# Six second-stage units by seven products in place of three, in a one-core attention layer

## The chip, the cores and the metric

The kernel runs on one core of a Trainium2 chip. The metric is the device time of one execution in microseconds (us); lower is better. The engines that appear below are TensorE (PE in the profile: matrix products; PEld is its loading of weights), VectorE (DVE), ScalarE (ACT), GpSimd (POOL) and SyncE (SP), whose queue issues the DMAs.

## The reference

One layer of an encoder trunk over 2048 tokens of width 1024, in float32: RMSNorm, one input projection to queries, keys, values and a gate (1024 columns each, 16 heads of 64), neighbourhood attention, gating by SiLU, output projection, residual, final RMSNorm.

```python
h = rmsnorm(x, norm_0)
q, k, v, gate = split(h @ w_in_0, 4)            # 2048 x 1024 each
# tokens form a 32 x 64 grid; a query sees the 8 rows x 16 columns around it
s = q . k / 8 + rpb_0[head, row offset, column offset]   # others: -1e30
o = softmax(s) @ v
x = x + (o * silu(gate)) @ w_out_0
return rmsnorm(x, norm_f)
```

`rmsnorm(x, g)` is `x * rsqrt(mean(x*x) + 1e-6) * g`. The factor `rsqrt(...)` belongs to a token, `g` to a column of x.

## The kernel before

**Precision.** Each float32 operand of a product is split into a high part (a rounded copy, made by ScalarE) and a low part (the operand minus the copy, made by VectorE). A product a*b is then three matmuls: high*high, high*low, low*high. `split_to` and `use_item` make such splits; a tile is mostly 128 x 512.

**Seven products.** The input projection of queries, keys and gate (`q`, `k`, `g`) is cut into 12 units (three kinds, four column groups j). In `seven_products` a unit is a 2 x 2 block product by Strassen's scheme in Winograd's form: seven block products of 12 matmuls each (84), line 421, in place of eight (96). It needs sums of weight blocks (`sum_`, line 410), sums of input blocks (T1 to T4, made once for all units), the splits of both (`form`, lines 403 and 404), and sums of results (`keep`, `add`, `out_`: lines 428, 432, 438). `form` runs six products ahead of the matmul that uses it. x blocks are named by their place: B11, B21, B12, B22, where the second digit is the block of 512 tokens.

**The norm.** x is multiplied by g (`g0`, per partition) when it is split. The token factor is applied to the results: `rb[c]`, a 128 x 512 tile made by `diagonal` and `spread_rstd`, is multiplied in by `evac` (VectorE, lines 326 and 328) for a plain result and by `out_` (POOL, line 439) for a summed one; for values `evac_v` takes it as a scale (line 377).

**The stages.**
- Stage one (to 326 us): the values of the first 1024 tokens, then all 12 units of `q`, `k`, `g` for those tokens by seven products (`stage_one`).
- Stage two (326 to 471 us): the values of the other 1024 tokens (`pair`), then three units (j = 0) by seven products (`stage_two`, `units_two`).
- Stage three: 64 attention steps (`scores`, `normalise`, `turns`, `values`), each for two of the four column blocks of a pair of heads `p` and a band of rows `T`. The 16 steps of band 0 come first, then 32 of bands 1 and 2, then 16 of band 3. Between them TensorE is fed with filler: first the remaining nine units in plain form (`projections`, lines 365, 367, 369; `halves` is their order), then the output projection (`outputs`, lines 1223 to 1227).

**A step.** The order of the instructions is written out by hand; each engine works its own queue in order. Step i does: `begin` (POOL adds position bias and mask to tables `em`, line 945, six sums when the head pair or band type changes; loads for later steps are queued), `feed` (filler matmuls), `middle`, `feed`, `normalise` of step i-1 (reciprocal on VectorE, line 979; scaling on POOL, line 981), `turns` of step i-2 (transposes, line 986; copies to `pta` on VectorE and ScalarE, lines 1011 and 1010), `scores` of step i (line 963; VectorE adds the table and finds the minimum, line 970; ScalarE takes the exponential, line 973) and `values` of step i-2 (line 1031). After the second half of a head pair the result is multiplied by the gate (`og`, line 1045) and stored. The amount of filler is fixed:

```python
early = 96 * (12 - len(units_two)) + 192
amount = [early / 48] * 48 + [(384 - 30) / 18] * 18
```

so a step in the first 48 has (96 x 9 + 192)/48 = 22 matmuls of filler. The loop over the steps is

```python
    for i in range(N + 2):
        a = amount[i]
        begin(i)
        feed(a * 0.45)
        middle(i)
        feed(a * 0.55, 8)
        if 0 < i <= N:
            normalise(i - 1)
        if i > 1:
            turns(i - 2)
        ...
        if i < N:
            scores(i)
        if i > 1:
            values(i - 2)
```

`later_loads(fs, lag, step)` issues loads that many filler matmuls later.

**Splits in the steps.** Filler needs splits of weights (`use_item`, line 178; output weights line 183). The queries of a step are split by `split_q` (line 499), gated results by `split_og` (line 1104). Four blocks of x that stage two overwrites are loaded and split again at the start of stage three (lines 155 and 156).

## Time and profile before

| | us |
|---|---|
| median of 3 runs | 1101.96 (1101.08 to 1102.29) |
| the profiled execution | 1102.79 |
| its span, first to last instruction | 1101.0 |
| mean granted clock of TensorE | 0.99 |

In the profile an engine's busy time is the union of its instructions. A group's row reads: line, engine, operation, output <- inputs, shapes, count | busy us, mean ns of one | idle time of the engine just before them and what ended it. Matmuls overlap, so their mean is longer than their distance. A row of waits reads: who <- for whom: total us, times, longest.

### The profile page before, as it was taken

How to read it: one execution, taken by the hardware profiler on the slowest of the kernel's cores; microseconds unless marked ns; L12 is line 12 of the kernel's file. 1: busy time of each engine (PE TensorE's matmuls, PEld its weight loads, DVE VectorE, ACT ScalarE, POOL GpSimd, SP SyncE). 2: the span in 40 equal slices, each digit the busy share in tenths (PEclk: the TensorE clock that was granted, in tenths of full speed). 3: DMA queues.
4: the chain of work that ended last, by engine and by line, in shares of the span. 5: the costliest groups of instructions: out<-in, count | busy, mean ns of one | idle time of the engine just before them, and what ended most of it. 6: DMA issues, size and time to landing. Idle time of an engine off the chain costs nothing.

```text
span 1101.0 us, 22543 instructions
## 1 busy us (share of the span) xinstructions
PE 1080.7 (98%) x7657; PEld 883.6 (80%) x7657; DVE 732.7 (67%) x1663; ACT 531.5 (48%) x1336; POOL 378.5 (34%) x483
## 2 busy tenths in 40 slices
PE   9999999999999999999999999999999999999997
PEld 6888888888888888877888888888877888887885
DVE  5376778788777337575665766665777777776644
ACT  7545343343344433255554554564556555555422
POOL 0000312222130001245445444424447666675200
PEclk9999999999999999998999999999999999999999
DMA  8633545454574235587767878687979797887452
GB/s 307 209 96 105 185 132 181 143 173 112 166 216 138 80 89 157 195 263 232 233 193 241 251 223 230 211 268 222 259 237 286 228 288 225 252 274 211 152 153 77
DMA packets 142962, 217.29 MB, mean 197 GB/s; under 512 B 18048, under 2 KB 65408, under 8 KB 142848
## 3 DMA queue, kind: packets, MB, share of 16 engines
q1 hardware_dynamic: 142704, 215.58, 64.6%
q8 instruction: 62, 1.02, 0.4%
q14 instruction: 52, 0.43, 0.1%
q10 hardware_dynamic: 144, 0.26, 0.1%
HBM read 157.05 MB, written 58.72 MB: 196 GB/s over the span
## 4 chain that ended last, share of the span: by engine, by line
PE 88%; DVE 5%; DMA 3%; issue 2%; ACT 1%; POOL 1%; SPq 0%; DVEq 0%; POOLq 0%
PE pp L421 24%; PE pv L534 16%; PE o L1031 7%; PE s L963 6%; PE pp L369 6%; PE pp L367 6%; PE pp L365 5%; PE po L1227 5%; PE po L1223 4%; PE po L1225 4%; PE ph L986 4%; ACT x L973 1%; PE zp L1242 1%; DVE gl L1104 1%; DMA sgt<-sgd 0%
## 5 line engine op out<-in xcount | busy, mean ns | idle before, releaser
L981 POOL TENSOR_SCALAR x<-x,st 128x360 f32<-128x360 f32 (+5 forms) x256 | 143.1, 579 | 239.1 <-DVE st L979 157.1
L439 POOL TENSOR_TENSOR tmp<-tmp,rb 128x512 f32<-128x512 f32 x45 | 73.5, 1634 | 399.2 <-DVE tmp L438 358.4
L973 ACT ACTIVATE x<-x,st 128x360 f32<-128x360 f32 (+5 forms) x256 | 151.8, 594 | 56.4 <-DVE st L970 56.4
L421 PE MATMUL pp<-h,f 128*128 128x512 f32 x480 | 155.4, 389 | 0.0
L945 POOL TENSOR_TENSOR em<-e,mk 128x480 f32<-128x480 f32 (+5 forms) x160 | 140.8, 915 | 5.0 <-DVE st L970 5.0
L421 PE MATMUL pp<-t,f 128*128 128x512 f32 x540 | 129.8, 389 | 0.1
L970 DVE CUSTOM_DVE_ANT_0 x<-s,em 128x360 f32<-128x360 f32 (+5 forms) x256 | 123.8, 538 | 5.1 <-PE s L963 2.0
L421 PEld LDWEIGHTS pp<-t,f 128*128 128x128 f32 x540 | 101.3, 188 | 21.5 <-DVE u L432 0.6
L369 PE MATMUL pp<-h,w 128*128 128x512 f32 x288 | 115.9, 403 | 0.0
L367 PE MATMUL pp<-l,w 128*128 128x512 f32 x288 | 114.2, 397 | 0.0
L365 PE MATMUL pp<-h,w 128*128 128x512 f32 x288 | 113.6, 394 | 0.0
L1010 ACT ACTIVATE pta<-ph 96x256 f32<-96x256 f32 (+1 forms) x224 | 58.8, 333 | 105.8 <-PE ph L986 105.8
L1031 PEld LDWEIGHTS o<-pta,vt 96*64 96x64 f32 (+2 forms) x1792 | 86.0, 139 | 24.2 <-DVE pta L1011 10.2
L421 PEld LDWEIGHTS pp<-h,f 128*128 128x128 f32 x480 | 90.1, 188 | 18.8
L1031 PE MATMUL o<-pta,vt 96*64 96x128 f32 (+4 forms) x1792 | 95.2, 258 | 7.5 <-DVE pta L1011 4.6
L1227 PE MATMUL po<-wol,gh 128*128 128x512 f32 x252 | 101.4, 403 | 0.0
L1223 PE MATMUL po<-woh,gh 128*128 128x512 f32 x252 | 100.0, 397 | 0.0
L1225 PE MATMUL po<-woh,gl 128*128 128x512 f32 x252 | 99.7, 395 | 0.0
L1011 DVE COPY pta<-ph 128x384 f32<-128x384 f32 (+3 forms) x128 | 60.5, 513 | 51.5 <-PE ph L986 51.2
L421 PE MATMUL pp<-l,f 128*128 128x512 f32 x240 | 93.4, 389 | 0.0
L534 PE MATMUL pv<-wh,h 128*128 128x512 f32 x256 | 88.1, 390 | 0.0
L534 PE MATMUL pv<-wh,l 128*128 128x512 f32 x256 | 88.0, 389 | 0.0
(136 smaller groups left out, 1951.1 us busy)
## 6 DMA issues: line engine op xcount, KB each, us to landing
raw<-in_wg_dram SPq DMA_DIRECT2D x126, 256.0 KB
e<-in_rpb_dram SPq DMA_DIRECT2D x54, 240.0 KB
vt<-vd SPq DMA_DIRECT2D x256, 48.0 KB
row<-in_xr_dram SPq DMA_DIRECT2D x32, 256.0 KB
vd<-v SPq DMA_DIRECT2D x32, 256.0 KB
k_hi<-hi SPq DMA_DIRECT2D x32, 256.0 KB
k_lo<-lo SPq DMA_DIRECT2D x32, 256.0 KB
qd<-tmp SPq DMA_DIRECT2D x32, 256.0 KB
```

The lines of the kernel that those rows point to most:

```text
L365: nc.tensor.matmul(p, wh[w, b][:, cols], hh[k, c], start=(k == 0), stop=False)
L367: nc.tensor.matmul(p, wh[w, b][:, cols], hl[k, c], start=False, stop=False)
L369: nc.tensor.matmul(p, wl[w, b][:, cols], hh[k, c], start=False, stop=(k == NK - 1))
L421: nc.tensor.matmul(B[n, P], t[:, int(m == 2), c], x[k][int(m == 1)], start=P in (1, 6, 5) and k == 0 and m == 0, stop=k == 3 and m == 2, s ...
L534: nc.tensor.matmul(ps[t], a[:, o], b, start=k == 0 and m == 0, stop=k == NK - 1 and m == 2)
L945: (nc.gpsimd if attending[0] or not s else nc.vector).tensor_tensor(sh(t), E[p, s][:, u0 + 4:u1 + 4, v0 + 8:v1 + 8], sh(MK[0][:, m0:m0 + n ...
L973: nc.scalar.activation(X[i, C][s], X[i, C][s], AF.Exp, bias=st[:, s:s + 1], scale=-1.0, accum_out=st[:, 2 + s:3 + s])
L981: nc.gpsimd.tensor_scalar(X[i, C][s], X[i, C][s], st[:, 4 + s:5 + s], 0.5, op0=OP.mult, op1=OP.mult)
L1031: nc.tensor.matmul(o[s * 64:s * 64 + 64, C * 128 + q0:C * 128 + q0 + nq], vt[C][:k, g - g0_, s * 64:s * 64 + 64], t[:k, at:at + nq], start ...
L1223: nc.tensor.matmul(p, gh, woh[q, j], start=(i == 0), stop=False)
L1225: nc.tensor.matmul(p, gl, woh[q, j], start=False, stop=False)
L1227: nc.tensor.matmul(p, gh, wol[q, j], start=False, stop=(i == NK - 1))
```

## The change

- `units_two` holds j = 0 and 1: six units go by seven products in stage two, six stay in plain form. `halves` starts at j = 2. A step in the first 48 now has (96 x 6 + 192)/48 = 16 matmuls of filler.
- For the second 1024 tokens the token factor is multiplied into the x blocks before they are split and summed: the new `normed` (VectorE, one instruction with `g` and `rb`). Eight such multiplications stand in stage one (`norms`: two in the third-last unit, six in the second-last), eight in stage two, four at the start of stage three. For this `diagonal` and `spread_rstd` of blocks 2 and 3 come earlier, and the loads of x11 and x21 too.
- The results for these tokens then need no factor: `out_` leaves out POOL's multiplication, the plain result goes from PSUM to `give` without `evac`, `evac_v` scales by 1.0, and `flush` and `pending` go. The sums T1 to T4 lose their factors and one ScalarE copy each.
- The gate is kept in plain order; the product `og` reorders it while reading.
- `split_og` runs ahead only where `quiet` says that POOL has no table sums; the query split moves to the step before, into the odd steps. `qr` has a tile of another pool.
- Loads in a step: `vt` first, then bias tables, keys later, the gate last.

```diff
-    units_two = [(k, j) for j in range(1) for k in "kqg"]
-    halves = [(k, j, 1, c) for j in range(1, 4) for g in (("k", "q", "g") if j < 3 else ("k", "qg")) for c in (2, 3) for k in g]
+    units_two = [(k, j) for j in range(2) for k in "kqg"]
+    halves = [(k, j, 1, c) for j in range(2, 4) for g in (("k", "q", "g") if j == 2 else ("k", "qg")) for c in (2, 3) for k in g]
...
         if kind == "x":
-            split_x(a, b, t, (hh[a, b], hl[a, b]))
+            normed("x%d1" % (a // 4 + 1), b, a % 4, t)
+            split_to(hh[a, b], hl[a, b], t, None)
...
-    def give(kind, hp, c, tmp):
+    def give(kind, hp, c, t, psum=False):
...
         if kind == "q":
-            store(("q", hp, c), 12, lambda: nc.sync.dma_start(qd[hp][:, s], tmp))
+            if psum:
+                o = ev([128, 512], F32, "q")
+                nc.scalar.activation(blocked(o), tiled(t), AF.Copy)
+                t = o
+            store(("q", hp, c), 12, lambda: nc.sync.dma_start(qd[hp][:, s], t))
             return
...
             nc.vector.tensor_tensor(lay(tmp), of(B[n, P]), of(u), OP.add)
-            nc.gpsimd.tensor_tensor(lay(tmp), lay(tmp), of(rb[c]), OP.mult)
+            if c0 == 0:
+                nc.gpsimd.tensor_tensor(lay(tmp), lay(tmp), of(rb[c]), OP.mult)
...
+    def normed(f, c, k, t):
+        nc.vector.scalar_tensor_tensor(t, t, gain(f, k), rb[c], op0=OP.mult, op1=OP.mult)
...
+            if (n, i) == (-3, 1):
+                diagonal(2)
+            if (n, i) == (-3, 3):
+                spread_rstd(2)
+            if (n, i) in norms:
+                f, k = norms[n, i]
+                normed(f, 2, k, L2[f][k])
+            if (n, i) == (-3, 4):
+                diagonal(3)
...
+        norms = {(-2, 3): ("x11", 0), (-2, 5): ("x11", 1), (-1, 0): ("x11", 2), (-1, 1): ("x11", 3),
+                 (-1, 3): ("x21", 0), (-1, 4): ("x21", 1), (-1, 5): ("x21", 2), (-1, 6): ("x21", 3)}
...
                 for k in ks:
-                    split_to(*X2[f][k], x[k], gain(f, k))
+                    normed(f, 3, k, x[k])
+                    split_to(*X2[f][k], x[k], None)
...
-                    y = ev([128, 512], F32, "y")
                     a, b, c = x11[k], x12[k], x22[k]
-                    nc.scalar.activation(y, b, AF.Copy, scale=gain("x12", k))
+                    nc.vector.tensor_tensor(c, c, b, OP.subtract)
                     nc.vector.tensor_tensor(b, b, a, OP.subtract)
-                    nc.vector.scalar_tensor_tensor(c, c, gain("x22", k), y, op0=OP.mult, op1=OP.subtract)
-                    nc.vector.scalar_tensor_tensor(a, a, gain("x11", k), c, op0=OP.mult, op1=OP.add)
+                    nc.vector.tensor_tensor(a, a, c, OP.add)
...
                 p = yield from group(w, a, c, n)
-                pending.append((c, lambda kind=kind, hp=2 * j + a, c=c, p=p: evac(kind, hp, c, p)))
-                flush(c)
+                state["event"] = clock[0]
+                give(kind, 2 * j + a, c, p, True)
...
-            nc.vector.tensor_tensor(og, o, SG.pop((p, T)), OP.mult)
+            nc.vector.tensor_tensor(blocked(og), blocked(o), tiled(SG.pop((p, T))), OP.mult)
...
-            if n < ready["loaded"] and place[n] <= k + 1 and clock[0] - loaded_at[n] >= 28 and whole(n):
+            near = 2 if quiet[0] else 1 if i >= 4 else 0
+            if n < ready["loaded"] and place[n] <= k + near and clock[0] - loaded_at[n] >= 28 and whole(n):
                 split_og(n)
...
     def begin(i):
         all_loads()
         m = i // 2
+        if 0 < i <= N:
+            p, T, cs = pairs[i - 1]
+            later_loads(load_v(p, T, cs[0]) + load_v(p, T, cs[1]), 0, 1.25)
...
-                LOADS[m + 1] = kh, _, kl = load_qk(*nx)
-                later_loads([kh, kl], 0, 2)
+                kh, q, kl = load_qk(*nx)
                 if nx[0] != p:
-                    later_loads(load_e(nx[0]), 4, 2)
-        if 0 < i <= N:
-            p, T, cs = pairs[i - 1]
-            later_loads(load_v(p, T, cs[0]) + load_v(p, T, cs[1]), 1, 1.5)
+                    later_loads(load_e(nx[0]), 6, 2)
+                later_loads([kh, kl], 10, 3)
+                NEXT.append(q)
...
-            later_loads([lambda: load_sg(p, T)], 7, 0)
+            later_loads([lambda: load_sg(p, T)], 15, 0)
 
     def middle(i):
...
-        if type(QT[order[m]]) is not tuple:
-            split_q(*order[m])
-        if m + 1 < len(order):
-            later_loads([LOADS[m + 1][1]], 1, 0)
+        if i % 2 and m + 1 < len(order):
+            split_q(*order[m + 1])
+        elif i % 2 == 0 and NEXT:
+            later_loads([NEXT.pop()], 0, 0)
...
-        feed(a * 0.45)
+        feed(a * 0.25)
+        quiet[0] = i % 2 == 1 or i >= N
+        feed(a * 0.2)
         middle(i)
         feed(a * 0.55, 8)
+        quiet[0] = i >= N
```

More of the change, by code (lines that the diff above doesn't have):

```diff
@@ L595, in also @@
                     for k in (0, 1):
-                        split_to(*X2["B11"][k], L2["x11"][k], gain("x11", k))
+                        split_to(*X2["B11"][k], L2["x11"][k], None)
                 elif i == 1:
-                    L2["x21"] = [p([128, 512], F32, "land") for p in (mp, mp, ep, ep)]
-                    for k in range(4):
-                        load_x(2, "x21", k, L2["x21"][k])
                     for a, b in ((1, 1), (0, 2), (1, 2)):
@@ L1228, in outputs @@
                 yield 1
-                ahead(k)
+                ahead(k, i)
             while k >= ready["res"]:
```

71 lines of the change are left out of this document (30 added, 41 removed).

## The prediction

> **What bounds the kernel now.** I read the page first: the busy shares, the granted clock and the chain.
>
> ```profile
> span 1101.0 us, 22543 instructions
> PE 1080.7 (98%) x7657; PEld 883.6 (80%) x7657; DVE 732.7 (67%) x1663; ACT 531.5 (48%) x1336; POOL 378.5 (34%) x483
> ...
> PE 88%; DVE 5%; DMA 3%; issue 2%; ACT 1%; POOL 1%; SPq 0%; DVEq 0%; POOLq 0%
> ```
>
> TensorE has work in 98% of the span and holds 88% of the chain that ended last. The next busiest engine, VectorE, is at 67%. So a removed matmul is removed time wherever TensorE stays fed, and the question is where it does not. For that I read the waits of TensorE, longest first:
>
> ```profile
> PE o L1031 <- DVE pta L1011: 4.6, 5, 2.0
> PE o L1031 <- DMA vt<-vd: 1.9, 2, 1.6
> ...
> PE s L963 <- DVE tmp L326: 1.5, 1, 1.5
> PE s L963 <- ACT pta L1010: 1.2, 1, 1.2
> ```
>
> All real waits lie in the attention stage. Then the busy times by stretch (columns: PE, PEld, DVE, ACT, POOL busy; granted clock; DMA share; GB/s):
>
> ```profile
> 288.00:307.00 19.00, 19.00 (x85) 15.76 (x84) 14.82 (x20) 6.37 (x11) 4.84 (x4) 1.00 0.50 166
> 307.00:326.00 19.00, 19.00 (x85) 15.73 (x84) 14.36 (x21) 10.02 (x18) 4.81 (x4) 1.00 0.86 264
> 326.00:348.00 22.00, 22.00 (x99) 18.22 (x98) 17.00 (x28) 10.96 (x19) 2.20 (x2) 1.00 0.59 156
> ```
>
> ```profile
> 462.00:515.00 53.00, 50.02 (x338) 40.02 (x338) 37.32 (x88) 26.25 (x72) 26.08 (x35) 0.94 0.83 262
> 515.00:605.00 90.00, 90.00 (x843) 73.79 (x840) 52.14 (x162) 45.46 (x148) 46.24 (x76) 1.00 0.74 224
> ...
> 715.00:810.00 95.00, 94.74 (x954) 76.77 (x952) 62.22 (x161) 52.35 (x154) 43.44 (x60) 1.00 0.85 248
> 810.00:910.00 100.00, 95.78 (x945) 78.61 (x946) 75.80 (x207) 59.85 (x173) 60.34 (x79) 0.97 0.85 262
> ```
>
> Up to 462 us TensorE is full at clock 1.00. In the attention stage it is full too, but for three places: the entry (462 to 515: idle 3.0 us, clock 0.94), the turn from projections to outputs (810 to 910: idle 4.2 us, clock 0.97), and one late wait for `vt` (below).
>
> **What one matmul and one step cost.** The chain in order of time, and TensorE's timeline in a step:
>
> ```profile
> 182.01 144.45 PE pp L421 x636
> ...
> 514.33 1.26 PE o L1031 x24
> 522.62 1.26 PE o L1031 x24
> ...
> 757.11 1.49 PE o L1031 x32
> 766.33 1.49 PE o L1031 x32
> ```
>
> ```profile
> 600.01 0.39 PE L367 MATMUL pp<-l,w 128*128 128x512 f32 x1
> ...
> 603.41 0.39 PE L367 MATMUL pp<-l,w 128*128 128x512 f32 x1
> ```
>
> A row's duration (0.39 us) overlaps the next row; what counts is the distance of starts. By the first row it is 144.45/636 = 0.227 us for a product of the seven, and by the last two (603.41 - 600.01)/15 = 0.227 us for a plain one. An attention step runs from one `o` to the next: 8.29 us in the first 16 steps (row band 0), 9.22 us in the following 32 (bands 1 and 2).
>
> **Term 1, the matmuls.** Three more units in seven products are 3 x 84 = 252 matmuls where the plain groups had 3 x 96 = 288. So 36 fall away: 36 x 0.227 = 8.2 us. The built programs agree: 1260 becomes 1512 at the seven-product line, 864 becomes 576 at the plain lines, and nothing else changes on TensorE. That is gained if everything else still hides. What moves: stage two gets longer by 252 x 0.227 = 57.2 us, and each of the first 48 steps loses 6 of its 22 fillers, 1.36 us of cover. A step becomes 6.9 us (band 0) or 7.9 us (bands 1, 2).
>
> **Term 2, VectorE in stage one.** Eight multiplications by norm factor and `rb` move into the third- and second-last unit (two and six), and the diagonals of blocks 2 and 3 with them. The groups of instructions give their prices, alone and beside POOL's 1.63 us multiplies:
>
> ```profile
> L439 POOL TENSOR_TENSOR tmp<-tmp,rb 128x512 f32<-128x512 f32 x45 | 73.5, 1634 | 399.2 <-DVE tmp L438 358.4
> L410 DVE TENSOR_TENSOR raw<-raw,s 128x512 f32<-128x512 f32 x15 | 24.5, 1635 | 0.0
> L410 DVE TENSOR_TENSOR raw<-raw 128x512 f32<-128x512 f32 x15 | 10.3, 686 | 0.0
> L693 DVE SCALAR_TENSOR_TENSOR land<-land,g 128x512 f32<-128x512 f32 x4 | 3.0, 752 | 0.1
> ```
>
> `L410` is the fair sample: the same sort of sum takes 0.69 us alone and 1.63 us where it regularly meets the POOL multiply. So a multiplication costs 0.75 us (the nearest row, the last) to 0.75 + 0.95 = 1.70 us. Six of them add 4.5 to 10.2 us to the 14.8 busy in 288 to 307, against 19 us. The low end just fills the unit; the high end leaves 6 us over, for which the last unit (307 to 326) has 4.6 us free and the forms of the products are made six products (6 x 12 x 0.227 = 16 us) ahead. I take nothing on the path, 0 to 5 us as bounds.
>
> The Trainium skill (SBUF — State Buffer, Who interferes with whom) says that a VectorE instruction with two SBUF inputs and a GpSimd instruction that reads SBUF exclude each other, the second to issue waiting out the first whole. That speaks against these multiplications, which have two SBUF inputs while POOL still multiplies. By that rule the upper price is 0.75 + 1.63 = 2.38 us, and six would run 10 us over the unit; the 1635 of `L410`, 0.95 us over its free price, is less than a whole 1.63 us wait, so the trace shows contention but not the full block on average.
>
> **Term 3, stage two.** The eight multiplications for blocks 12 and 22 put 8 x 0.75 = 6 us into 326 to 348, where VectorE has 5 us free; the sums of T1 to T3 behind them, done there in part, slide into the next stretch, and block 22 is wanted only after 348 us. In the six units POOL multiplies no more (9 x 1.63 us off POOL, and with it the meeting above), and the evacuations' multiplications go. Nothing on the path, 0 to 1 us.
>
> **Term 4, the attention steps.** What VectorE must do before the next `pta` copies sets whether `o` waits. The timeline at 804 to 812 us shows how that fails:
>
> ```profile
> 804.24 6.39 POOL L945 TENSOR_TENSOR em<-e,mk 128x360 f32<-128x360 f32 x6
> 806.91 1.72 DVE L499 SCALAR_TENSOR_TENSOR ql<-qr,qh 128x512 fp32r<-128x512 f32 x1 [1.13 <-ACT qh L498]
> 808.55 2.63 DVE L1104 TENSOR_TENSOR gl<-ograw,gh 128x512 fp32r<-128x512 f32 x2
> 811.10 0.21 DVE L979 RECIPROCAL st<-st 128x2 f32<-128x2 f32 x2
> 811.24 0.99 DVE L1011 COPY pta<-ph 96x384 f32<-96x384 f32 x2
> 811.83 1.38 PE L1031 MATMUL o<-pta,vt 96*64 96x128 f32 x26 [2.04 <-DVE pta L1011]
> ```
>
> Three splits beside POOL's table sums take 4.35 us, and the reciprocal and `pta` copies queue behind them: TensorE waits 2.04 us. In the built program of after, the query split stands in the steps without table sums, `gl` mostly there too, and the multiplications of plain evacuations are gone from VectorE. Of the seven steps 4 to 16 that have sums, four keep the `og` product alone between softmax and reciprocal, and none has over four operations; before it was up to six. VectorE's load is 52.14/90 x 8.29 = 4.8 us a step before, and less than that in 6.9; ACT has 45.46/90 x 8.29 = 4.2, POOL 46.24/90 x 8.29 = 4.3. None of the three becomes the bound. Some steps keep four operations beside sums, and seven or ten stand in two steps of the turn to the outputs (ten there before as well): I take +3 us of new small waits, 0 to 8.
>
> **Term 5, the three old holes.** Each costs its idle time and its lost clock: at the entry 3.0 + 0.06 x 53 = 6.2 us, at the turn 4.2 + 0.03 x 100 = 7.2 us. The late `vt`:
>
> ```profile
> 1000.00:1050.00 50.00, 48.04 (x418) 39.18 (x416) 28.97 (x88) 22.41 (x64) 19.36 (x29) 0.97 0.62 187
> ```
>
> 1.6 us of wait (the row of waits) and 0.03 x 50 = 1.5 us of clock. After issues the `vt` loads first in a step, ahead of keys and tables on SP's queue, and closer together, so I count this hole closed: -3 us. At the turn the two `gl` splits beside sums move out but ten operations remain in one step: I count -3 of 7.2. At the entry four blocks of x are split on VectorE:
>
> ```profile
> L156 DVE SCALAR_TENSOR_TENSOR l<-raw,g,h 128x512 fp32r<-128x512 f32 x4 | 4.5, 1154 | 0.0
> ```
>
> Now each takes a multiplication and a difference, 0.75 + 0.69 us, where `L156` took 1.15; POOL is free of its multiplies there, and TensorE arrives with 15 fewer fillers in the first step: no change, -6 to +6.
>
> The Trainium skill (TensorE: Matmul & The Clock Gate, Part 1) has the array at half clock after an idle window of about 3.4 us. By that rule the holes of 2 us would cost only themselves; here the clock falls to 0.94 and 0.97 in just the stretches whose longest wait is 2.0 us, so the rows price a hole at nearly twice its length, and I use the rows.
>
> **The sum.** -8.2 (matmuls) + 0 + 0 + 3 (small waits) - 3 (`vt`) - 3 (turn) = -11.2 us. The profiled execution took 1102.79 us, its span 1101.0 with 1.8 around it; it lies 0.8 above the median of 1101.96. So 1102.8 - 11.2 = 1091.6 profiled, 0.8 less for the median: 1091.
>
> **The rivals.** *All holes close* and no new ones open: -8.2 - 6.2 - 7.2 - 3.1 = -24.7, or 1077; half the way there from the forecast is the likely case, 1084. For it: the reordering takes aim at just these waits. Against: the ten operations and the crowded entry stay. Chance 0.13.
>
> *VectorE binds stage one*: the term's 5 us reach the products of stage two's start, 1096. For it 78% busy in 288 to 307 and the multiply still on POOL; against, sixteen microseconds of lead. Chance 0.10.
>
> *Shorter steps open new holes* in the entry and the turn, each with its lost clock: two of 2 + 1.7 us, 1098. For it: 1.36 us less cover in each step. Chance 0.10.
>
> *DMA becomes the bound of bands 1 and 2, slower than before.* 715 to 810 shows 0.85 of the DMA engines busy, 0.85 x 9.22 = 7.8 us a step. The fillers' share of that is small:
>
> ```profile
> raw<-in_wg_dram SPq DMA_DIRECT2D x126, 256.0 KB
> ```
>
> 48 plain matmuls need two such weight tiles and write two to four result tiles of the same size, some 1.2 MB; 6/48 of that at 248/0.85 = 292 GB/s is 0.5 us. 7.3 us in a step of 7.9 is a share of 0.93, and the highest of these stretches is 0.86. If it cannot rise over that, a step lasts 7.3/0.86 = 8.5 us, 0.6 more than TensorE needs; over 32 steps that is 20 us, -8.2 + 20: 1114. It decides from a share of about 0.9 on: there the step is 8.1 us, +8 us over the 32, and the gain is gone. Against it: only 1.9 us in all were spent waiting for `vt` in the whole run at 0.85, since loads are issued a step or more ahead. Chance 0.14, and 0.03 that the effects cancel. That the change doesn't do what it says is excluded by the built program's counts.
>
> **The numbers.** Forecast 0.50, the rivals 0.13, 0.10, 0.10, 0.14, and 0.03 for the cancelling. About 0.2% is what a measurement of this kernel can tell from no change: 2.2 us. Faster: 0.50 + 0.13 + 0.10 + 0.08 = 0.81 (0.02 of the new holes' 0.10 end within it); the same: 0.02 + 0.03 = 0.05; slower: 0.14. The range leaves out the DMA case and little below: 1080 (holes closed) to 1104.
>
> **What would show it.** Right: 1512 seven-product matmuls at 0.227 us, stage two ending near 57 us later (about 528 us), steps near 6.9 and 7.9 us, no `vt` wait late, clock 1.00 at 840 to 1000. Wrong: a `pta`, `vt` or `kt` wait that recurs in bands 1 and 2 with the DMA share near 0.9, TensorE idle between 288 and 350, or an entry with more than 3 us idle.

## The result, and the profile after

The changed kernel is slower: 1150.86 us median (1149.63 to 1151.93, 4 runs) against 1101.62 us (1101.08 to 1102.29, 4 runs) for the kernel before on the same chip, a ratio of 1.0446 with a 95% interval of 1.0428 to 1.0464. The forecast was 1091 us, the range 1080 to 1104. Each ratio below compares a run's median with that of the kernel before on the same chip; a bracket behind a time holds the ratio and its 95% interval.

The page of the profiled execution, with the same parts as before and the chain by line:

```profile
span 1148.1 us, 22479 instructions
PE 1095.5 (95%) x7621; PEld 890.6 (78%) x7621; DVE 725.6 (63%) x1680; ACT 535.5 (47%) x1354; POOL 359.4 (31%) x474
...
PE 77%; DMA 9%; DVE 4%; ACT 3%; SPq 3%; issue 2%; POOL 1%; DVEq 0%; ACTq 0%; POOLq 0%
...
PE pp L409 27%; PE pv L529 15%; PE o L1035 6%; PE s L967 5%; DMA qr<-qd 5%; PE po L1233 4%; PE po L1229 4%; PE po L1231 4%; PE ph L990 3%; PE pp L357 3%; PE pp L355 3%; PE pp L353 2%; SPq L924 1%; DMA raw<-in_w_out_dram 1%; DMA xr<-in_x_dram 1%
```

No engine's share of the span is higher than before. What changed is the chain: TensorE fell from 88% to 77% of it, DMA rose from 3% to 9%, and one load, the queries, holds 5% by itself.

The first two stages went as forecast. The timeline by stretch (start, end and length in us, then busy time of PE, PEld, DVE, ACT, POOL; granted clock; DMA share; GB/s) and two pieces of the chain in order of time:

```profile
288.00:307.00 19.00, 19.00 (x86) 15.74 (x85) 18.09 (x26) 6.37 (x11) 4.14 (x3) 1.00 0.29 105
307.00:326.00 19.00, 19.00 (x86) 15.74 (x85) 17.33 (x23) 10.12 (x18) 5.58 (x4) 1.00 0.69 213
326.00:348.00 22.00, 22.00 (x98) 18.20 (x97) 15.27 (x24) 8.19 (x14) 1.69 (x2) 1.00 0.48 125
```

```profile
413.68 111.53 PE pp L409 x492
527.95 0.69 DVE l L491
```

VectorE is filled to 18.1 of 19 us by the new multiplications, TensorE stays full in all three rows. A product of the seven still takes 111.53/492 = 0.227 us, and stage two ends at 528 us, 57 later than before.

The loss is in the attention steps. I cut them where the transposes of steps 0, 16, 36, 48 and 63 start. A stretch that begins at step n begins at its transposes. The first fence is the kernel before, the second the changed kernel:

```profile
492.00:630.00 138.00, 134.73 (x1239) 109.53 (x1238) 84.68 (x252) 72.40 (x229) 72.44 (x115) 0.98 0.76 229
630.00:808.00 178.00, 177.88 (x1817) 145.13 (x1818) 115.22 (x307) 96.93 (x285) 79.77 (x112) 1.00 0.80 237
808.00:919.00 111.00, 106.56 (x1063) 87.10 (x1059) 84.65 (x229) 65.70 (x193) 69.45 (x91) 0.97 0.83 254
919.00:1041.00 122.00, 119.13 (x1137) 97.70 (x1137) 84.52 (x267) 65.69 (x190) 69.80 (x102) 0.99 0.77 233
```

```profile
545.00:675.00 130.00, 119.06 (x1145) 95.65 (x1144) 68.29 (x235) 71.56 (x231) 72.31 (x115) 0.95 0.77 225
675.00:852.00 177.00, 163.55 (x1705) 130.92 (x1705) 105.06 (x293) 98.54 (x292) 82.39 (x116) 0.96 0.81 237
852.00:955.00 103.00, 96.73 (x1005) 76.91 (x999) 70.59 (x213) 58.07 (x179) 65.63 (x88) 0.95 0.79 235
955.00:1087.00 132.00, 121.70 (x1124) 99.61 (x1123) 81.37 (x267) 65.22 (x190) 68.53 (x102) 0.96 0.75 219
```

In the second fence TensorE is idle for 41 of 542 us where it had been idle for 11 of 549, and the clock is 0.95 to 0.96 where it had been 0.97 to 1.00. Yet the data comes no faster than before (219 to 237 GB/s against 229 to 254). The times, with one decimal from the starts of the transposes:

| stretch, us | before | forecast by Term 1 | after | units alone (below) |
|---|---|---|---|---|
| up to the first transposes | 492.1 | 545.2 | 545.0 | 545.6 |
| steps 0 to 15 | 137.9 | 116.1 | 130.2 | 124.6 |
| steps 16 to 35 | 177.5 | 150.3 | 176.5 | 169.0 |
| steps 36 to 47 | 111.8 | 99.6 | 103.3 | 100.7 |
| steps 48 to 62 | 121.3 | 121.3 | 132.3 | 123.5 |
| the rest | 60.4 | 60.4 | 60.8 | 60.4 |
| span | 1101.0 | 1092.9 | 1148.1 | 1123.8 |

The forecast column takes 1.36 us from each step that has 16 fillers in place of 22 (3 of these 48 stand before the first transposes). So 45 x 1.36 = 61 us were to come back in the three stretches behind the first transposes, and 44 of them did not; 11 more were lost in the last 15 steps, whose number of fillers did not change.

The views of waits name who stood still, and for what (the first two views are of the whole run, the third is SP's from 560 to 1000 us):

```profile
PE s L967 <- ACT pta L1014: 24.7, 16, 5.4
PE s L967 <- DVE y L1140: 6.6, 2, 4.8
```

```profile
ACT qh L493 <- DMA qr<-qd: 69.9, 18, 7.7
```

```profile
SPq L924 <- DMA kt<-k_lo: 27.9, 23, 2.8
SPq L924 <- DMA kt<-k_hi: 17.0, 18, 2.0
SPq L924 <- DMA sgt<-sgd: 14.2, 23, 1.1
```

One such place in the timeline (rows between them left out):

```profile
713.49 0.37 SPq L904 DMA_DIRECT2D qr<-qd  x1
...
718.27 2.17 SPq L924 DMA_DIRECT2D vt<-vd  x3
719.72 0.63 ACT L493 ACTIVATE qh<-qr 128x512 fp32r<-128x512 f32 x1 [7.66 <-DMA qr<-qd]
...
721.78 0.96 ACT L1014 ACTIVATE pta<-ph 128x256 f32<-128x256 f32 x4
722.36 1.17 PE L967 MATMUL s<-kt,qh 64*128 64x480 f32 x3 [5.38 <-ACT pta L1014]
```

SP's queue runs late, so the query load is issued at 713.5 and its split starts only at 719.7. ScalarE has waited for it 7.7 us, and the copies to `pta` stand behind the split in ScalarE's queue; the scores wait for those, 5.4 us. SP itself waits above all for transfers: in the built program the DMAs on SP's queue use eight semaphores in turn, so each waits until the one eight places before it has landed.

### The profile page after: what moved, and what is told of

Same layout as the page of the kernel before. It is cut to its first block, busy times and chain, and to the rows that moved or that the text cites. A ratio compares the mean times of both kernels' runs of the same rounds, so it can differ in the third digit from the quotient of the medians.

```text
span 1148.1 us, 22479 instructions
## 1 busy us (share of the span) xinstructions
PE 1095.5 (95%) x7621; PEld 890.6 (78%) x7621; DVE 725.6 (63%) x1680; ACT 535.5 (47%) x1354; POOL 359.4 (31%) x474
## 4 chain that ended last, share of the span: by engine, by line
PE 77%; DMA 9%; DVE 4%; ACT 3%; SPq 3%; issue 2%; POOL 1%; DVEq 0%; ACTq 0%; POOLq 0%
PE pp L409 27%; PE pv L529 15%; PE o L1035 6%; PE s L967 5%; DMA qr<-qd 5%; PE po L1233 4%; PE po L1229 4%; PE po L1231 4%; PE ph L990 3%; PE pp L357 3%; PE pp L355 3%; PE pp L353 2%; SPq L924 1%; DMA raw<-in_w_out_dram 1%; DMA xr<-in_x_dram 1%
## 5 line engine op out<-in xcount | busy, mean ns | idle before, releaser
L409 PE MATMUL pp<-h,f 128*128 128x512 f32 x576 | 186.6, 389 | 0.0
L409 PE MATMUL pp<-t,f 128*128 128x512 f32 x648 | 155.9, 390 | 0.4 <-DVE u L420 0.2
L428 POOL TENSOR_TENSOR tmp<-tmp,rb 128x512 f32<-128x512 f32 x36 | 58.8, 1633 | 270.2 <-DVE tmp L426 230.2
L409 PEld LDWEIGHTS pp<-t,f 128*128 128x128 f32 x648 | 121.5, 188 | 26.3 <-DVE u L420 1.2
L409 PEld LDWEIGHTS pp<-h,f 128*128 128x128 f32 x576 | 108.2, 188 | 22.3
L967 PE MATMUL s<-kt,qh 64*128 64x480 f32 (+5 forms) x512 | 91.7, 381 | 35.3 <-ACT pta L1014 24.7
L409 PE MATMUL pp<-l,f 128*128 128x512 f32 x288 | 112.1, 389 | 0.0
L967 PEld LDWEIGHTS s<-kt,qh 64*128 64x128 f32 x512 | 53.5, 191 | 49.1 <-ACT pta L1014 33.3
L494 DVE SCALAR_TENSOR_TENSOR ql<-qr,qh 128x512 fp32r<-128x512 f32 x32 | 22.8, 713 | 103.4 <-ACT qh L493 101.6
L529 PE MATMUL pv<-wl,h 128*128 128x512 f32 x256 | 88.0, 389 | 0.0
```

The lines of the kernel that those rows point to most:

```text
L409: nc.tensor.matmul(B[n, P], t[:, int(m == 2), c], x[k][int(m == 1)], start=P in (1, 6, 5) and k == 0 and m == 0, stop=k == 3 and m == 2, s ...
L428: nc.gpsimd.tensor_tensor(lay(tmp), lay(tmp), of(rb[c]), OP.mult)
L529: nc.tensor.matmul(ps[t], a[:, o], b, start=k == 0 and m == 0, stop=k == NK - 1 and m == 2)
L967: nc.tensor.matmul(pst[s], qq[a, qs], kk[a, :r1 - r0, c0:c1], start=(m == 0), stop=(m == 2))
```

## The experiments

Two things could be to blame: the three more units by seven products, which leave fewer fillers in a step (the *units*), or the three edits of the steps: the order of loads, the query's load and split, the output splits held to quiet steps.

### The step edits, taken back one at a time

First in the changed kernel. Query as before:

```diff
-            QT[p, T] = t = lp([128, 512], F32, "qr")
+            QT[p, T] = t = qp([128, 512], F32, "qr")
...
-        if i % 2 and m + 1 < len(order):
-            split_q(*order[m + 1])
-        elif i % 2 == 0 and NEXT:
-            later_loads([NEXT.pop()], 0, 0)
+        if i % 2 or i >= N:
+            return
+        if type(QT[order[m]]) is not tuple:
+            split_q(*order[m])
+        if NEXT:
+            later_loads([NEXT.pop()], 1, 0)
```

> The changed kernel with one part undone: the queries of a pair of heads are again loaded two steps before they are split, and split in the middle of the even step that uses them. Load order, quiet splits and the six units stay. Theory Q (the query load has one short step of lead, and ScalarE's in-order queue stands behind its landing): the 70 us that ScalarE waits for the query tile go, and the time falls from 1151 to about 1100, between 1092 and 1108. Rival L (the new order of the loads overfills SyncE's queue, queries are only where it shows): the wait moves to another load, keys or values, and the time stays over 1125. Rival D (steps of 7 us are too short for the DMA traffic whatever the order): over 1125 too.

Order of loads as before:

```diff
-        if 0 < i <= N:
-            p, T, cs = pairs[i - 1]
-            later_loads(load_v(p, T, cs[0]) + load_v(p, T, cs[1]), 0, 1.25)
...
+                later_loads([kh, kl], 0, 2)
                 if nx[0] != p:
-                    later_loads(load_e(nx[0]), 6, 2)
-                later_loads([kh, kl], 10, 3)
+                    later_loads(load_e(nx[0]), 4, 2)
...
+        if 0 < i <= N:
+            p, T, cs = pairs[i - 1]
+            later_loads(load_v(p, T, cs[0]) + load_v(p, T, cs[1]), 1, 1.5)
...
-            later_loads([lambda: load_sg(p, T)], 15, 0)
+            later_loads([lambda: load_sg(p, T)], 7, 0)
```

> The changed kernel with the other part undone: keys, tables, values and gate are loaded in the old order and at the old lags; the queries keep the short lead and the split in the odd step. Theory Q: ScalarE still waits for the query tile; the time stays over 1125. Rival L: most of the loss goes, about 1100 to 1110. Rival D: over 1125.

Query load at the head of the even step, ahead of the values:

```diff
+        if i % 2 == 0 and m + 1 < len(order):
+            kh, q, kl = load_qk(*order[m + 1])
+            later_loads([q], 0, 0)
```

> The changed kernel with the query load moved to the head of the even step, ahead of the eight value loads, half a step earlier; everything else as changed, the split stays in the odd step. Theory Q: the load lands some 8 us earlier in the queue's order, the ScalarE wait goes almost entirely, 1088 to 1100. Rival L: the value loads now come later in a queue that is overfull, waits move to them, 1115 to 1150. Rival D: over 1125.

And the new place of the query load and split in the kernel before (the first diff turned round, except that the load keeps its lag of one filler):

> The kernel before with one part of the change alone: the queries are split one step after their load is queued, in the odd step, with their landing tile in the other pool. Steps keep 22 fillers. Theory Q: the lead is one long step of 8.3 to 9.2 us and the load stands earlier in the queue; some waits, 1102 to 1115. Rivals L and D: 1098 to 1104, no loss, since queue and step length are those of before.

Measured: 1153.28 us (ratio 1.0468, 1.0444 to 1.0491), 1144.56 (1.0391, 1.0365 to 1.0418), 1142.98 (1.0366, 1.0333 to 1.0398), and in the kernel before 1114.68 (1.0116, 1.0091 to 1.0142). In the changed kernel the late query is not the cause by itself: with the old query the time does not fall. Another load is late then; the longest wait of VectorE with the old query, then with the early one:

```profile
DVE og L1049 <- DMA sgt<-sgd: 63.6, 16, 7.2
```

```profile
DVE og L1049 <- DMA sgt<-sgd: 77.9, 25, 7.0
```

With the query moved, the factors `sgt`, whose load the changed kernel puts last in a step, are what VectorE waits for longest. I read this as a queue that is behind as a whole.

### Is it the number of loads?

The value loads are eight a step. The four of each column block were merged into one, in both kernels; and in the kernel before ten were made of eight, by halving the first of each four:

```diff
-            nc.sync.dma_start(VT[p, T, C][r * w:r * w + w, :g1_ - g0_].rearrange("p g d -> p (g d)"), src[r])
...
-        return [lambda r=r: rows(r) for r in range(4)]
+            nc.sync.dma_start(t[:4 * w, :g1_ - g0_].rearrange("p g d -> p (g d)"), src)
+        return [rows]
```

> The changed kernel with the four value loads of a column block (one for each four grid rows) issued as one DMA of the same bytes: two value DMAs in a step instead of eight, everything else as changed. Theory N (after the first runs: each DMA of SyncE's queue waits for the one eight places before it, so the number of DMAs, not their bytes, sets how fast loads arrive; both kernels issue about 1.5 to 1.6 DMAs a microsecond in the attention stage): six of some 13 DMAs a step go, whichever load was late is in time, and the time falls to 1085 to 1105. Rival D (the bytes bind: too short a step for the traffic): no change worth the name, over 1135.

> The kernel before with the same merging of value loads. Theory N: it was near the limit, but its waits for loads were 2 us in all, so 1094 to 1102. Rival D: 1098 to 1104.

> The kernel before with the suspected cost raised: one of the four value loads of a column block is cut in two, so ten value DMAs in a step instead of eight, same bytes. Theory N: at 0.63 us a DMA a step of 8.3 to 9.2 us needs 1.3 us more of the queue; the slack that before has is used up and the time rises by 15 to 80 us, to 1115 to 1180. Rival D: the bytes are the same, 1098 to 1106.

Measured: 1179.68 us (1.0705, 1.0681 to 1.0729), 1142.05 (1.0362, 1.0339 to 1.0385) and 1127.05 (1.023, 1.02 to 1.026). All three are slower, so fewer loads are not by themselves faster. Merged loads move less, not more. Changed kernel with merged loads, 680 to 860 us, and SP's longest wait in the whole run:

```profile
680.00:860.00 180.00, 158.01 (x1595) 126.27 (x1592) 95.48 (x276) 92.39 (x274) 72.08 (x103) 0.92 0.70 222
```

```profile
SPq L923 <- PE o L1034: 120.4, 48, 6.7
```

A merged load holds SP until the buffer is free, with all that is queued behind it. But the kernel before is sensitive: two loads more a step, at the same bytes, cost it 24 us. It had less room than its 1.9 us of `vt` waits let me believe. A limit on bytes alone does not explain these 24 us; they stay unexplained.

### The units alone

The first two diffs above together, and the output splits not held:

```diff
-            near = 2 if quiet[0] else 1 if i >= 4 else 0
+            near = 1
```

> The changed kernel with the attention steps' other edits undone together: queries with the old lead and split, loads in the old order, the splits of gated results placed as before. What is left is six units by seven products, the norm in the blocks and 16 fillers a step. Theory N: the queue has the same number of DMAs in shorter steps, so the loss stays: 1130 to 1155. If the retimed loads and splits were the cause (rivals Q and L together), 1092 to 1105.

Measured: 1127.53 us (1.0241, 1.0207 to 1.0274). So the units cost 25 us without any of the step edits, where 8 us less were forecast: 33 us to explain. (The norm in the blocks, the plain results read from PSUM and the gate in plain order are still in this kernel; no run takes them apart from the units.) By stretch, and TensorE's longest wait:

```profile
546.00:670.00 124.00, 116.00 (x1136) 94.09 (x1133) 69.66 (x229) 70.95 (x228) 70.89 (x112) 0.94 0.77 233
670.00:839.00 169.00, 158.69 (x1695) 129.14 (x1693) 105.92 (x296) 99.81 (x295) 82.69 (x116) 0.96 0.86 251
839.00:940.00 101.00, 94.40 (x1011) 75.64 (x1011) 73.67 (x213) 57.44 (x177) 66.06 (x88) 0.97 0.83 241
```

```profile
PE o L1035 <- DMA vt<-vd: 16.7, 11, 2.9
```

A step of the middle row needs 251 GB/s x 169 us / 20 = 2.12 MB. In the 150.3/20 = 7.5 us that TensorE would take, that is 282 GB/s. Of the four stretches of the kernel before shown above, the best has 254 GB/s. Cut into stretches of 50 us, its attention stage shows at most 264 GB/s, that of the units alone 262 (other starts find up to 271 and 272):

```profile
860.00:910.00 50.00, 49.39 (x505) 40.54 (x502) 41.16 (x121) 31.44 (x93) 33.23 (x43) 1.00 0.85 264
```

```profile
810.00:860.00 50.00, 44.71 (x459) 36.49 (x460) 31.52 (x84) 29.63 (x87) 28.58 (x38) 0.90 0.89 262
```

The middle stretch is 18.7 us late. The neighbours need 1.81 MB in 7.26 us = 249 GB/s and got 233 (8.5 us late), and 2.02 MB in 8.30 us = 243 and got 241 (1 us late). In these three stretches, the more the need, the later. Call this the data rate; its rival is that the chain of small operations in a step (minimum, exponential, reciprocal, copies) is what a shorter step does not cover.

Two things weaken the comparison. First, the turn from projections to outputs has changed its stretch. Before, it lay in steps 36 to 38, with the hole of 2.04 us that the prediction shows; here it lies in step 33, in the middle stretch:

```profile
810.12 0.89 PE L1035 MATMUL o<-pta,vt 128*64 128x128 f32 x16 [1.86 <-DMA vt<-vd]
813.93 1.55 PE L1035 MATMUL o<-pta,vt 96*64 96x128 f32 x16 [2.92 <-DMA vt<-vd]
815.41 0.80 PE L1229 MATMUL po<-woh,gh 128*128 128x512 f32 x1
```

These two waits are 4.8 of the 10.3 us that TensorE is idle in the middle stretch, so part of its 18.7 us belongs to the turn, and the next stretch looks better for having lost it. Second, 251 GB/s at a share of 0.86 is a mean over steps that differ widely. Steps 16 and 17 of the units alone:

```profile
670.20:677.70 7.50, 7.50 (x87) 6.16 (x86) 4.62 (x16) 4.29 (x14) 2.56 (x5) 1.00 1.02 333
677.70:685.60 7.90, 7.54 (x85) 6.12 (x84) 4.95 (x14) 4.13 (x13) 7.90 (x10) 1.00 0.61 161
```

(A transfer counts where it starts, so a short piece can show a share over 1.) So the DMA engines can do more than the mean for a step; how the loads are spread over the steps is a rival that no run tested.

### The fillers spread evenly

```diff
-    amount = [early / 48] * 48 + [(384 - 30) / 18] * 18
+    amount = [20.25] * 66
```

> The units alone, with the fillers spread evenly: 20.25 filler matmuls in each of the 66 attention steps, where the units-alone kernel has 16 in the first 48 and 19.7 in the last 18 and runs over 400 output matmuls (some 90 us) behind the last step at 77 to 160 GB/s. No instruction and no byte is added or removed. Theory D' (each step must last until its share of the data has come at about 240 GB/s; what is taken from the fillers is given back as waiting): the last step ends later, with hardly any waiting in the steps, the tail shrinks to about 45 us, and the kernel takes 1100 to 1112 instead of 1127.5. Rival S (the loss sits in the step itself, a chain of softmax copies that any shorter stage two would not touch): same waits in each step, 1127. Rival O (the output matmuls pulled ahead wait for their own loads): slower than 1127.

Measured: 1137.64 us (1.0328, 1.0308 to 1.0348), slower than the units alone: the third case, and for a reason that I had not seen. Outputs of band 1 are ready only when its last head pair is; the fillers ran out at 847 us and the steps up to 900 us had none:

```profile
851.00:900.00 49.00, 33.99 (x456) 29.18 (x452) 31.38 (x98) 27.91 (x89) 39.18 (x52) 0.73 0.85 239
```

```profile
PE o L1035 <- DMA vt<-vd: 11.8, 5, 2.9
```

```profile
900.43 1.82 PE L1035 MATMUL o<-pta,vt 96*64 96x128 f32 x32
912.10 0.80 PE L1229 MATMUL po<-woh,gh 128*128 128x512 f32 x1 [9.85 <-ACT gh L1107]
```

This tests the redistribution badly, but it shows steps without filler. The first row has TensorE idle for 15 of 49 us at a clock of 0.73, and the DMA engines at 0.85 and 239 GB/s. The second row, of the waits in the same stretch, puts 11.8 of these 15 us down to the value loads. From the values at 849.57 us to those at 900.43 us (third row) are seven steps, 7.3 us each, though TensorE's own work had shrunk by all 20 fillers, 4.6 us. A bare step brings 239 x 7.3 = 1.74 MB; the 0.38 MB to the 2.12 MB above, with 16 fillers, fit the prediction's estimate of what fillers bring and store (0.5 us at 292 GB/s for six). So without filler a step here is mostly as long as its data takes.

The last row is the wait for an output tile that had been asked for late.

### Fewer bytes

In the units alone, and as a control in the kernel before:

```diff
-            nc.sync.dma_start(t[:, :n].bitcast(F32), src[p][:, r0 * GW:r1 * GW])
+            k = n if src is k_hi else 120
+            nc.sync.dma_start(t[:, :k].bitcast(F32), src[p][:, r0 * GW:r0 * GW + k])
```

> The units alone, where the load of the low part of the keys brings 120 columns instead of 704 to 960, and the scores take the high part in its place. The number of loads, their order, and all matmuls stay; about 12 MB of some 117 MB fall away in the attention stage. Theory D': at 240 GB/s that is 49 us of transfer, so the waits shrink until TensorE binds again: 1090 to 1102, against 1127.5 with all bytes. Theory I (the time SP takes to issue a load, 0.43 us each, is the bound): the count is the same, so 1122 to 1128. Rival S (chain of copies in the step): 1127.

> The control: the kernel before with the same cut of the loads of the low keys. Theory D' with TensorE as the bound of the kernel before: at most the three old holes close, 1085 to 1100. If the cut gained here as much as with the units alone (25 us or more), it would not be the shorter steps that meet the data rate.

Then a second cut, of one table `e` in two as well:

```diff
-            nc.sync.dma_start(t, rpb[2 * p + s])
+            nc.sync.dma_start(t if s == 0 else t[:, :120], rpb[2 * p + s] if s == 0 else rpb[2 * p + s][:, :120])
```

> The units alone with the low keys cut to 120 columns and one of two tables e cut to 120 of 480 columns, the other used for both heads; some 16 to 17 MB less in the attention stage, at the same number of loads. Theory D' (bytes per step over TensorE's time per step): the first 12 MB took 21.7 us, and the rest of the waits are small; 1098 to 1104. If the first cut already brought the steps to their next limit (the chain of splits and copies): 1104 to 1107.

Measured: units alone 1105.85 us (1.0034, 1.0017 to 1.0052) after the first cut and 1098.62 (0.9977, 0.9959 to 0.9995) after the second; the kernel before 1094.46 (0.9935, 0.9917 to 0.9953). So 12 MB less takes 22 us off the units alone and 7 off the kernel before, with matmuls, loads and their order the same. The units alone gain three times as much as the control; the difference, some 14 us, is what the transfers cost the shorter steps. Neither the chain of small operations nor the time to issue loads can give that, since the cut changes neither. The steps after the second cut:

```profile
545.00:664.00 119.00, 114.98 (x1164) 93.05 (x1164) 70.79 (x234) 72.38 (x234) 71.93 (x115) 0.97 0.73 214
664.00:822.00 158.00, 152.59 (x1695) 124.46 (x1691) 107.10 (x298) 99.59 (x294) 83.21 (x116) 1.00 0.80 231
822.00:918.00 96.00, 92.78 (x1004) 75.14 (x999) 70.35 (x209) 56.90 (x176) 66.44 (x88) 0.96 0.75 224
```

The middle stretch now needs 231 x 158 / 20 = 1.82 MB in 7.5 us, 243 GB/s, and gets 231; the span of 1096.1 us is 3 over the forecast of 1092.9. The first cut gave less than its 49 us of transfer and less than was expected, and the rate that a stretch gets falls with the need, so a mean rate is not all of it. With the same first cut in both kernels the units still cost 11 us (1105.85 - 1094.46) where they had cost 25. The cut thus accounts for 14 of the 33 us by which the units missed the forecast; the other 20 (11, and the gain of 8 that did not come) are not shown to come from the transfers. The second cut, which has no control, brings the units alone just below the uncut kernel before.

### Another queue

```diff
-        nc.sync.dma_start(SG[p, T], sgd[p][:, T * 512:T * 512 + 512])
+        nc.gpsimd.dma_start(SG[p, T], sgd[p][:, T * 512:T * 512 + 512])
...
-            nc.sync.dma_start(t, rpb[2 * p + s])
+            nc.gpsimd.dma_start(t, rpb[2 * p + s])
```

> The units alone, with the loads of the tables e and of the factors sg (86 loads, some 21 MB) issued by POOL instead of SP. SP's loads wait for the load eight places before them; POOL's have places of their own, so more can be in flight, and SP has 86 fewer to issue. Theory D' in the form that the 16 DMA engines' rate is the bound: the bytes are the same, 1120 to 1130. Theory L (the eight places of SP's queue and its order are the bound, with engines at a share of 0.8): 1095 to 1115. POOL's issue costs could add some us to either.

Measured: 1126.34 us (1.022, 1.0185 to 1.0256), no gain over the units alone. Steps 16 to 35:

```profile
668.00:841.00 173.00, 159.17 (x1696) 128.91 (x1694) 105.76 (x298) 100.27 (x296) 93.54 (x138) 0.96 0.86 252
```

252 GB/s at a share of 0.86, as with one queue (251, 0.86). So taking 86 loads out of SP's eight places did not raise the mean rate. Nor is that mean a ceiling of the DMA engines. In 50 us of the same run they moved just the 282 GB/s that the shorter steps needed:

```profile
793.00:843.00 50.00, 46.61 (x489) 37.55 (x485) 35.03 (x93) 32.73 (x95) 29.35 (x44) 0.97 0.94 282
```

The Trainium skill (DMA: Bandwidth & Descriptors, Rules for kernel authors) says that spreading DMAs over issuing engines brings no bandwidth, since all run on the same 16 engines; the mean rate of this run agrees. The same table advises to join small transfers into large ones; the merged value loads above were slower, by 29 us in the changed kernel and 39 in the one before, so here the measurement decides against it for loads into buffers that come free late.

### Fewer bytes in a kernel that computes everything

Keys are stored and loaded once, and split where they are used:

```diff
+    def split_k(p, T):
+        l, h = KT[p, T], kp([128, 960], F32R, "kt")
+        n = (KEY_ROWS[T][1] - KEY_ROWS[T][0]) * GW
+        split_to(h[:, :n], l[:, :n], l[:, :n].bitcast(F32), None)
+        KT[p, T] = [t.rearrange("p (r c) -> p r c", c=GW) for t in (h, l)]
...
+        if i % 2 and m + 1 < len(order):
+            split_k(*order[m + 1])
```

> The kernel before, with the keys stored and loaded once as full-precision numbers and split into high and low part where they are used (one copy on ScalarE, one difference on VectorE over 704 to 960 columns, in the odd steps), in place of two parts stored and loaded. The result is the same. It takes 32 loads (14 MB) and 32 stores (8 MB) away, and adds about 0.6 us a step to ScalarE and VectorE. Theory D' (each step needs its data at no more than some 250 GB/s; the kernel before is near that in bands 1 and 2): 1092 to 1098, since leaving out 12 MB gave 1094.5. Rival S (the chain of small VectorE and ScalarE operations in a step is what hurts): slower than before, 1103 to 1110.

> The same edit of the keys on the units alone. Theory D': leaving out 12 MB took 1127.5 to 1105.9; 14 MB of loads and some 6 MB of stores less give 1096 to 1106. Rival S: 1127 or more.

Measured: the kernel before 1098.74 us (0.9959, 0.9943 to 0.9975), the units alone 1107.16 (1.0039, 1.0022 to 1.0056). The first is a little faster than both kernels of this case. Both lie about 1 us over what was expected. With whole keys in both kernels the units still cost 8 us (1107.16 - 1098.74), where the matmuls were to gain 8.2; so 17 of the 33 us went with the keys' bytes. The split may have a price of its own: its VectorE half waits for ScalarE's (units alone, VectorE's longest wait), though no run shows what that does to the time:

```profile
DVE kt L490 <- ACT kt L489: 45.1, 26, 3.0
```

### The step edits without the units

All three in the kernel before (the diffs of the changed kernel's `begin`, `middle`, `ahead` and loop, without those of the units), the held output splits alone on the units alone, and the order of loads alone in the kernel before:

```diff
 units alone, splits held
-            near = 1
+            near = 2 if quiet[0] else 1 if i >= 4 else 0
 kernel before, order of loads
-                later_loads([kh, kl], 0, 2)
+                later_loads([kh, kl], 10, 3)
...
-            later_loads([lambda: load_sg(p, T)], 7, 0)
+            later_loads([lambda: load_sg(p, T)], 15, 0)
```

> The kernel before with the three edits of the attention steps alone (loads of values first, keys and tables later; query loaded in one even step and split in the next odd one; output splits held to steps without table sums), without the three units. If these edits cost time by themselves: 1114 to 1125 (the query edit alone gave 1114.7). If they cost only where the steps are short: 1099 to 1104. They were put at 0 in the prediction, but for -6 us at vt and the turn: 1096.

> The units alone, but with the output splits held to steps without table sums as in the changed kernel. The changed kernel is 23 us over the units alone; taking back the query edit alone gave +2, the load edit alone -6. If the held splits are the rest: 1142 to 1148. If the three only hurt together, or the query and the loads do: 1126 to 1130.

> The kernel before with the changed kernel's order of loads alone (values at the head of the step, tables and keys 6 to 13 matmuls later, the factors sg later still); the query is loaded and split as before. All three edits of the steps cost 19 us (1122.5), the query edit alone 13 (1114.7), the held splits nothing. Theory Q (a late load is what costs: whatever stands behind the eight value loads and two 480 KB key loads comes late): the order alone costs 10 to 22 us, 1112 to 1124. Rival: the order is harmless with 22 fillers a step and the 19 us are the query's: 1100 to 1106.

Measured: 1122.50 us (1.0197, 1.0164 to 1.023), 1127.02 (1.0238, 1.0209 to 1.0267) and 1112.11 (1.0092, 1.0066 to 1.0119). Held splits cost nothing (1127.0 against 1127.5). The order of loads costs 10 us alone, the query edit 14 alone, all three 19, so singly they do not add up. In the changed kernel, taking the order back gave 6 us and taking the query back nothing. As two blocks, units and step edits do add up: 2.4% + 2.0% make 4.4%, and the changed kernel is at 4.5%. The 10 us of the order lie in the last stretch, from 919.6 to 1051.5 us, 131.9 us for steps 48 to 62 against 121.3 before:

```profile
920.00:1051.00 131.00, 124.50 (x1116) 101.14 (x1112) 81.81 (x272) 65.18 (x192) 67.34 (x102) 0.95 0.74 221
```

That is where the changed kernel lost its 11 us, too. At 221 GB/s and a share of 0.74, less than the kernel before had there (233, 0.77), the mean rate does not explain it. I take it for lateness (the gate's load moved from 7 to 15 fillers behind the step's start, keys from 0 to 10), but no run took these loads one by one.

## Why the prediction was wrong

**Term 1 (matmuls)** was right in its counts and prices: 0.227 us, stage two ending at 528 us. The step that failed is the sentence behind it, "That is gained if everything else still hides", which gave each of 48 steps 1.36 us: the six fillers' cover was put at nothing. With the units alone, 28 of the 61 us that were to come back did not (8.5, 18.7 and 1.1 us in the three stretches), and the median was 25 us over the kernel before in place of 8 under it. The removed filler was cover. For 14 to 17 of these 33 us the runs with fewer bytes show that it covered transfers; what the rest covered stays open.

**The rival "DMA becomes the bound"** came nearest, and had 0.14. It put a step at 8.5 us if the share cannot rise over 0.86, and in steps 16 to 35 the units alone show 0.86 and 169.0/20 = 8.45 us. That agreement is in part luck: the share did rise over 0.86, to 0.94 for 50 us and 1.02 for a step, and some of the 8.45 us is the turn's. The 1114 us that the rival gave lie 37 under the result; it had no price for the step edits and none for band 0. What made me give it so little was "only 1.9 us in all were spent waiting for `vt`". Waits are no measure of room. A better measure is bytes per step over the time that the step is to have. From the rows that I had quoted that was (248 GB/s x 9.22 us - 0.15 MB)/7.9 us, some 270 GB/s, against at most 262 in the attention rows. I also left band 0 out, whose share was lower; its steps were to become the shortest, 6.9 us, and it came 8.5 us late.

**Term 4 (steps)** had +3 us for small waits. The query edit was counted as relief, since the split moved to steps without table sums; its load was not costed at its new place. Alone it costs 14 us in the kernel before. The held splits alone neither cost nor bring anything (1127.0 against 1127.5).

**Term 5 (holes)** had -3 us for the value loads, now first in the step. The `vt` wait did close, but the order alone costs 10 us. The queue is one, and what steps ahead puts something else behind; that this is the cause was not shown load by load. Terms 4 and 5 together were to gain 3 us (+3 - 3 - 3); their edits cost 19 us in the kernel before and 23 on top of the units (1150.9 against 1127.5). These 26 and the 33 of Term 1 are nearly all of the 60 us between forecast and result.

**Terms 2 and 3 (VectorE in stages one and two)** were right at 0: TensorE is full from 288 to 348 us, though VectorE rose to 18.1 of 19. A new multiplication took 0.75 us in the median and 1.79 at most, near the 0.75 to 1.70 of the prediction.

**The price of a hole** by the clock held: after, 41 us idle and some 24 us of lost clock (0.04 to 0.05 of 542) stand against 11 and 7 before. So a hole cost some 1.6 times its length, though the row of `pta` waits has a mean of 24.7/16 = 1.5 us; the rule that I had set against it (TensorE: Matmul & The Clock Gate, Part 1, of the Trainium skill: an idle window of about 3.4 us) would let most of these waits cost themselves alone.

Stays open: what holds the mean of a long stretch at 250 GB/s and a share of 0.86. The Trainium skill (DMA: Bandwidth & Descriptors, Specifications) has 435 GB/s as the ceiling of the fabric; no stretch of the attention stage shown here came near it. The 250 are no hard limit either: the page of the kernel before, in slices of 27.5 us, has single ones at up to 288 in the attention stage.

```profile
GB/s 307 209 96 105 185 132 181 143 173 112 166 216 138 80 89 157 195 263 232 233 193 241 251 223 230 211 268 222 259 237 286 228 288 225 252 274 211 152 153 77
```

The 11 or 8 us that the units cost with the same bytes taken out of both kernels, and the gain of 8 that did not come, were not taken apart; the uneven load of the steps, waits between splits as in the row of `kt` above, and the norm in the blocks are candidates. Of the query edit's 14 us in the kernel before, no single wait carries them. An even spread of the fillers that keeps to what is ready was not tried.

## What to carry to other kernels

Before shortening a stage that hides transfers, divide its bytes by the time it is to have, stretch by stretch, and compare with the best rate that the same stage has shown over a stretch as long; few waits before the change only say that the stage was long enough. Work moved out of such a stage can be paid for twice: once where it goes, and again where it is missing. When one queue carries all loads, a load moved ahead moves the others back, so cost the last one too.

## What the runs showed of the hardware

- In the stretches of 100 to 180 us shown here the attention stage moved at most 254 GB/s, at shares of 0.70 to 0.86, and moving 86 loads to POOL's queue did not change the mean (252, 0.86). Shorter pieces moved more: 282 GB/s at 0.94 for 50 us, 333 at 1.02 for one step.
- Of two, eight and ten value loads a step, eight were fastest: ten cost 24 us, two cost 29 and 39.
- In the run with evenly spread fillers, steps without filler took 7.3 us for 1.74 MB each, at a TensorE clock of 0.73.
